# A two-layer hybrid decoder trunk on one core: paired recurrence blocks, weight slots out of turn, another load order at the start

## The chip, the cores and the metric

One core of a Trainium2 chip runs the whole program. The metric is device time in microseconds (us) from start to end. The kernel before was timed in three runs: median 1348.71 us (1348.5 to 1348.83). The profiled execution that all rows below come from took 1349.72 us.

## The reference, cut to what matters

Two layers of a trunk over 512 tokens of width 1024, all in float32. Each layer normalizes, projects the input once, sends the columns to three mixers (a chunked gated recurrence with 4 heads, latent attention, sparse attention with the 128 best keys per query), projects their outputs, adds the residual, and runs a squared-ReLU MLP of width 4096.

```python
for l in range(DEPTH):
    u = rms_norm(h, attn_norm_w[l])
    proj = u @ w_in[l]
    ...
    y_hgrn = hgrn2_mixer(hq, hf, hi, hg, lb_all[l], hgrn_norm_w[l])
    y_mla = mla_mixer(...)
    y_dsa = dsa_mixer(...)        # top-128 keys per query by an index score
    mixed = jnp.concatenate([y_hgrn, y_mla, y_dsa], axis=-1)
    h = h + mixed @ w_out[l]
    u = rms_norm(h, mlp_norm_w[l])
    h = h + jnp.square(jax.nn.relu(u @ w_mlp_in[l])) @ w_mlp_out[l]
return rms_norm(h, final_norm_w)
```

## The kernel before, in words

Activations lie transposed in eight blocks of 128 channels by 512 tokens (`h[0..7]`). A float32 product with weights is made of three products in the fast format fp32r: every operand is split into a high part (`whi`, a cast of the loaded tile `raw`, on ScalarE or VectorE) and a rest (`wlo`, a subtraction on VectorE). Weights stream through five buffers each of `raw`, `whi` and `wlo`.

Nothing is issued while the program is written: `Recorder` collects every operation with an estimated duration (`_Engine.cost`), and `order()` plans all engines at once. `forward()` is a list scheduler: at each step it takes the engine that is free first and gives it the ready operation with the most work behind it; `backward()` renews these levels from the plan just made. Twelve such rounds are run and the shortest plan is written out, so the order on every engine's queue is the planner's. Buffers are named by tags (`CAPS` says how many of each: `mm` 3 and `mx` 5 are PSUM banks, `un` 24 are general 128x512 tiles in SBUF). `RESERVE` says how many buffers of a tag must stay free before one may be taken out of its turn; 9 means strictly in turn, which holds for `raw`, `whi`, `wlo` and `mm`.

SyncE (SP) issues the loads in one queue: a load that waits for its buffer holds all behind it. The places that matter here:

- **Start** (`setup`, `vectors`): three products of zeros run on TensorE, four parts of x are loaded into `wlo` buffers, transposed by TensorE against the identity in `consts`, scaled with the first norm's rows (`an`, 16x128) and split into `u`. Positions and one norm's rows (`hnw`) are loaded from GpSimd's queue.
- **Recurrence** (`hgrn_head`, once per head and layer, 8 times): for each of four 128-token blocks, the block of products K1 x Q1 goes to the PSUM tile `pa`, and its upper right 64x64 quarter is then overwritten by Ks x Qs, a product of two 64-column operands in `hq`. VectorE copies the masked result to `at` (`copy_predicated`), TensorE multiplies `at` with the values.
- **Index top-k** (`index_topk`): 16 rounds of max and match_replace on VectorE for three query blocks, per layer.
- **Sparse attention and output projection** (`dsa_attend`, `layer`): for each of eight blocks m, 18 products over the first two mixers are accumulated in an `mm` bank, which VectorE then adds to the old `h[m]`; that was put away to DRAM (`hd[m]`) and is loaded back as `un<-d`. The sparse mixer's part (`mx<-pt` is its last product) follows in a second `mm` tile per block.

Of the kernel before, what the change touches and what calls it, by code (L numbers as in the profile page):

```python
# [22 lines left out]
DEPTH = 2  # L23
# [5 lines left out]
ROUNDS = 12  # L29
# [144 lines left out]
class Op:  # L174
    __slots__ = ("eng", "run", "dur", "lat", "preds", "succs", "bufs", "idx", "level", "left", "ready",
                 "start", "end", "window", "ways", "after", "lock")
# [7 lines left out]
class Recorder:  # L184
# [38 lines left out]
    def add(self, eng, run, outs, ins, dur, lat=0.0, lock=False):  # L223
        if self.ways is not None:
            self.ways.append((eng, run, outs, ins, dur, lat, lock))
            return None
        op = Op()
        op.lock = lock
        op.eng, op.run, op.dur, op.lat, op.idx = eng, run, dur, lat, len(self.ops)
        preds = set()  # L230
        for v in ins:
            box = v.box
            preds.update(i for i, b, w in v.buf.log if w and _meet(b, box))

        box_of = lambda v: None if eng == "PE" else v.box
        for v in outs:
            box = box_of(v)
            preds.update(i for i, b, w in v.buf.log if _meet(b, box))
        for v in outs:
            box = box_of(v)  # L240
            v.buf.log = [x for x in v.buf.log if not _within(x[1], box)] + [(op.idx, box, True)]
        for v in ins:
            if not any(v.buf is o.buf and _within(v.box, box_of(o)) for o in outs):
                v.buf.log.append((op.idx, v.box, False))
        op.bufs = list({id(v.buf): v.buf for v in list(ins) + list(outs)}.values())
        preds.discard(op.idx)
        op.window = WINDOW if lat and any(v.buf.tag in ("un", "lg") for v in outs) else 0
        op.preds, op.succs, op.ways = preds, [], None
        self.ops.append(op)
        return op  # L250

    def order(self):

        ops = self.ops
        for op in ops:
            for p in op.preds:
                ops[p].succs.append(op.idx)
        for op in reversed(ops):
            op.level = -(op.dur + op.lat + max((self.hop(op, ops[s]) - ops[s].level for s in op.succs), default=0.0))
        best = None  # L260
        for _ in range(ROUNDS):
            try:
                result, span = self.forward()
            except RuntimeError:
                if best is None:
                    raise
# [3 lines left out]
            self.backward(span)  # L270
        self.span, self.best = best[1], best[0]
        return [x[0] for x in best[0]]
# [45 lines left out]
    def forward(self):  # L318
# [25 lines left out]
        key = lambda op: (op.level, op.idx)  # L344
# [12 lines left out]
        while done < len(ops):  # L357
# [31 lines left out]
            for tag, bs in need.items():  # L389
# [4 lines left out]
                if len(s) - len(bs) < RESERVE.get(tag, 0) and max(turn[b] for b in bs) >= head[tag] + len(bs):  # L394
                    short = tag
                    break
# [39 lines left out]
            if op.lat:  # L436
                x = max(dma_free, t + 1100.0)
                dma_free = x + op.lat
                op.end = dma_free + 900.0
# [8 lines left out]
            for s in op.succs:  # L448
                o = ops[s]
                o.left -= 1  # L450
                o.ready = max(o.ready, op.end + self.hop(op, o))
# [20 lines left out]
class _Engine:  # L472
# [29 lines left out]
    def cost(self, method, named, views):  # L502
        v = dict(views)
        if method == "dma_start":
            shape = next(x for _, x in views).shape
            n = math.prod(shape) * 4
            return (60.0 if self.eng != "POOL" else 1000.0), max(100.0, n / 360.0)
        out = v.get("out") or views[0][1]
        if self.eng == "PE":
# [4 lines left out]
            if rhs.buf.r:  # L514
# [3 lines left out]
            return (130.0 if m <= 64 else 214.0), 0.0  # L518
        n = max(x.free for _, x in views)
        if self.eng == "ACT":  # L520
            d = 95.0 + n / 1.2
# [12 lines left out]
        if method == "reciprocal":  # L534
# [7 lines left out]
RESERVE = {"un": 8, "mx": 2, "t2": 2, "mm": 9, "raw": 9, "whi": 9, "wlo": 9, "sqa": 9, "rb": 9, "hw": 3, "hq": 2, "hS": 1,  # L542
           "lg": 9, "pt": 9, "u": 99}


class Build:
# [51 lines left out]
    def setup(self):  # L598
# [9 lines left out]
        nc.sync.dma_start(self.ident, a["consts"][:, 0:128])  # L608
# [8 lines left out]
        for i in range(4):  # L617
            nc.sync.dma_start(xin[i], a["x"][0, :, i * 256:(i + 1) * 256].rearrange("(t p) d -> p t d", p=128))
        self.vectors()
# [19 lines left out]

        for kt in range(KT):  # L640
# [7 lines left out]
    def vectors(self):  # L648
# [4 lines left out]
        for width, group in ((128, (("an", a["attn_norm_w"], 8),)),  # L653
# [7 lines left out]
            for key, ap, k in group:  # L661
                nc.sync.dma_start(rows[r:r + DEPTH * k, 0:width],
                                  ap.rearrange("l (k p) -> (l k) p", p=width) if k > 1 else ap)
# [9 lines left out]
        nc.gpsimd.dma_start(self.hnw, bass.AP(tensor=w.tensor, offset=w.offset, ap=[[0, 128], [128, DEPTH], [1, 128]]))  # L673
# [39 lines left out]
    def rope_tables(self):  # L713
# [3 lines left out]
        nc.gpsimd.dma_start(self.pos_i, bass.AP(tensor=pos.tensor, offset=pos.offset, ap=[[0, 128], [1, 512]]))  # L717
        self.pos_c = self.tile([128, 4], I32)
        nc.gpsimd.dma_start(self.pos_c, pos.rearrange("o (t p) -> p (o t)", p=128), allow_slow_non_contiguous=True)
# [795 lines left out]
    def hgrn_head(self, l, hd, hf, pq, vi, gate, cq, mix):  # L1515
# [187 lines left out]
```

## Time and profile before

| | us |
|---|---|
| median of three runs | 1348.71 |
| the profiled execution | 1349.72 |
| its span, first to last instruction | 1347.9 |
| TensorE busy | 1310.3 (97%) |
| VectorE busy | 1081.2 (80%) |
| ScalarE busy | 638.7 (47%) |
| mean granted TensorE clock | 0.988 |

The span has six stretches: the start to 15, the mixers of layer 0 to 310 and the rest of its output projection to 340, its MLP to 735, the same for layer 1 (mixers to 958, projection to 990), and the second MLP to 1338 with the last norm behind it. All planned operations carry one line, 491, so rows are told apart by tile names. A float32 matmul that isn't fp32r shows as two records. TensorE's ends are modelled: a stretch in which it shows as busy can still hold waits, and a gap in its row is a sure wait.

### The profile page before, as it was taken

To read this page: it belongs to the slowest core of one execution; us is meant where nothing else is said; L and a number is where in the kernel's file an instruction comes from. 1 tells how busy PE (TensorE), PEld (TensorE's weight loads), DVE (VectorE), ACT (ScalarE), POOL (GpSimd) and SP (SyncE) were. 2 spreads that over 40 slices of the span, in tenths; PEclk is the share of its full clock that TensorE was granted. 3 is DMA by queue.
4 is the path that set the end of the run, shared out by engine and by line. 5 is a ranking of instruction groups with operands and counts; after the bars stand their busy time and mean duration, and the time that the engine had idled before them with its cause. 6 is when DMAs were issued, how large, how long until landed. Compare 5 with 4: busy or idle time off the path is not lost.

```text
span 1347.9 us, 23357 instructions
## 1 busy us (share of the span) xinstructions
PE 1310.3 (97%) x9237; PEld 1185.5 (88%) x9237; DVE 1081.2 (80%) x2208; ACT 638.7 (47%) x1152; POOL 19.6 (1%) x34
## 2 busy tenths in 40 slices
PE   7999999998999999999999999999799999999996
PEld 5788788766999999999988887987599999999996
DVE  6999999984996777866666999999399777767765
ACT  5666636373553333433344684526255333433343
POOL 1010000000000000000010000000000000000000
PEclk8999999998999999999999999999899999999998
DMA  8540222333134332332463012224423223343321
GB/s 266 156 138 11 56 60 79 109 116 120 37 121 125 95 94 79 110 125 95 133 156 89 12 48 79 71 62 134 125 63 126 86 88 106 99 126 94 94 64 63
DMA packets 137106, 131.87 MB, mean 98 GB/s; under 512 B 14069, under 2 KB 129541, under 8 KB 136997
## 3 DMA queue, kind: packets, MB, share of 16 engines
q1 hardware_dynamic: 135716, 127.62, 31.1%
q0 software_dynamic: 1280, 2.77, 0.9%
q8 instruction: 72, 1.18, 0.4%
q14 instruction: 38, 0.30, 0.1%
HBM read 121.44 MB, written 8.92 MB: 97 GB/s over the span
## 4 chain that ended last, share of the span: by engine, by line
PE 88%; DVE 7%; DMA 2%; issue 1%; ACT 1%; SPq 0%; DVEq 0%; ACTq 0%
PE mm L491 58%; PE mx L491 29%; DVE un L491 3%; PE mx L1420 1%; DVE lg L491 1%; DVE wlo L491 1%; DMA wlo<-in_x_dram 1%; DMA un<-d 1%; DVE t L491 1%; DVE c L491 1%; DMA lg<-d 0%; ACT whi L491 0%; ACT t L491 0%; SPq L491 0%; ACT un L491 0%
## 5 line engine op out<-in xcount | busy, mean ns | idle before, releaser
L491 PE MATMUL mm<-un,whi 128*128 128x256 f32 (+1 forms) x2176 | 447.3, 295 | 14.8 <-DVE un L491 14.7
L491 ACT ACTIVATE whi<-raw 128x1024 fp32r<-128x1024 f32 (+2 forms) x232 | 240.6, 1041 | 413.4 <-PE mm L491 248.5
L491 PEld LDWEIGHTS mm<-un,whi 128*128 128x128 f32 x2176 | 344.5, 189 | 29.7 <-DVE un L491 16.7
L491 DVE TENSOR_TENSOR wlo<-raw,whi 128x1024 fp32r<-128x1024 f32 (+2 forms) x250 | 297.3, 1197 | 44.5 <-ACT whi L491 39.9
L491 PE MATMUL mm<-u,whi 128*128 128x512 f32 (+1 forms) x960 | 292.1, 366 | 2.1 <-DVE c L491 1.1
L491 PE MATMUL mm<-un,wlo 128*128 128x256 f32 (+1 forms) x1088 | 275.3, 294 | 0.0
L491 PEld LDWEIGHTS mm<-u,whi 128*128 128x128 f32 x960 | 176.1, 189 | 29.4 <-issue 2.9
L491 PEld LDWEIGHTS mm<-un,wlo 128*128 128x128 f32 x1088 | 190.5, 189 | 6.1 <-issue 0.8
L491 DVE TENSOR_TENSOR un<-mm,un 128x512 f32<-128x512 f32 (+2 forms) x184 | 119.8, 662 | 91.2 <-PE mm L491 77.6
L491 PE MATMUL mx<-u,whi 128*128 128x256 f32 x736 | 189.9, 282 | 0.0
L491 PE MATMUL mm<-u,wlo 128*128 128x512 f32 (+1 forms) x480 | 159.5, 363 | 0.0
L491 PE MATMUL mm<-whi,u 128*128 128x256 f32 (+1 forms) x640 | 142.2, 305 | 0.2 <-DVE un L491 0.2
L491 PEld LDWEIGHTS mx<-u,whi 128*128 128x128 f32 x736 | 137.2, 188 | 0.0
L491 PEld LDWEIGHTS mm<-whi,u 128*128 128x128 f32 x640 | 103.1, 189 | 8.0 <-issue 4.5
L491 PE MATMUL mx<-lg,whi 128*128 128x256 f32 x448 | 107.7, 281 | 0.0
L491 PE MATMUL mx<-un,un 128*128 128x512 f32 (+4 forms) x380 | 104.5, 364 | 2.0 <-DVE un L491 1.5
L491 PE MATMUL mx<-u,wlo 128*128 128x256 f32 x368 | 102.3, 282 | 0.0
L491 PEld LDWEIGHTS mm<-u,wlo 128*128 128x128 f32 x480 | 89.0, 189 | 12.0 <-issue 0.4
L491 ACT ACTIVATE un<-t 128x512 fp32r<-128x512 f32 (+1 forms) x85 | 53.3, 628 | 66.1 <-DVE t L491 60.1
L491 PE MATMUL mm<-wlo,u 128*128 128x256 f32 (+1 forms) x320 | 83.0, 299 | 0.0
L491 PEld LDWEIGHTS mx<-un,un 128*128 128x128 f32 (+1 forms) x380 | 65.2, 188 | 18.9 <-DVE un L491 4.2
L491 PEld LDWEIGHTS mx<-lg,whi 128*128 128x128 f32 x448 | 79.6, 188 | 0.0
(200 smaller groups left out, 1960.5 us busy)
## 6 DMA issues: line engine op xcount, KB each, us to landing
raw<-in_w_mlp_in_dram SPq DMA_DIRECT2D x64, 512.0 KB, 3.8
raw<-in_w_mlp_out_dram SPq DMA_DIRECT2D x64, 512.0 KB, 4.1
raw<-in_w_in_dram SPq DMA_DIRECT2D x42, 512.0 KB, 3.7
d<-un SPq DMA_DIRECT2D x20, 256.0 KB, 2.5
raw<-in_w_in_dram SPq DMA_DIRECT2D x18, 256.0 KB, 3.1
raw<-in_w_out_dram SPq DMA_DIRECT2D x16, 256.0 KB, 2.7
raw<-in_w_out_dram SPq DMA_DIRECT2D x8, 512.0 KB, 3.4
un<-d SPq DMA_DIRECT2D x16, 256.0 KB, 4.6
```

Source lines behind the costliest of these rows:

```text
L491: real(*[res(v) for v in args], **{k: res(v) for k, v in kw.items()})
L1420: self.real.tensor.matmul(outs[i].get(), vals[i].get(), rhs[i].get(), start=k == 0, stop=k == NT - 1)
```

## The change

Part by part:

1. The recurrence's four 64x64 products per head become two of 128x128, each over two blocks at once, in a PSUM tile of their own, `pz` (tag `mx`). Only the wanted quarters are copied from it into `at`, by two copies after `copy_predicated`.
2. The planner may take `raw`, `whi` and `wlo` buffers out of turn while 2 to 4 stay free (`RESERVES`, tried in turn over 24 rounds), holds fewer of `un`, `t2` and `hq` back, and has new costs: 300 for a short float32 product (130 or 214 before), 20 more for ScalarE from SBUF, a slower and later end for loads, no hop between operations of TensorE. `SEED` is 0, so the random shifts of levels are off.
3. The identity, x part 0, the rows `an` and x part 1 go first in SP's queue, in this order. Parts 2 and 3, and the loads of positions and `hnw` (now on SP), are placed by the planner.
4. Three products without a use are written behind the loads: one of x part 0, two of x part 1.

```diff
-ROUNDS = 12
+ROUNDS = 24
+SEED = 0
...
-        for _ in range(ROUNDS):
...
+        for i in range(ROUNDS):
+            for reserve in RESERVES[i % 3:]:
+                try:
+                    result, span = self.forward(reserve)
+                    break
+                except RuntimeError:
+                    continue
...
-        key = lambda op: (op.level, op.idx)
+        key = lambda op: (op.level - op.early, op.idx)
...
-                op.end = dma_free + 900.0
+                op.end = dma_free + 2200.0
...
-                o.ready = max(o.ready, op.end + self.hop(op, o))
+                o.ready = max(o.ready, op.end + (0.0 if op.eng == o.eng == "PE" else self.hop(op, o)))
...
-            return (60.0 if self.eng != "POOL" else 1000.0), max(100.0, n / 360.0)
+            return (60.0 if self.eng != "POOL" else 1000.0), max(100.0, n / 310.0)
...
-            return (130.0 if m <= 64 else 214.0), 0.0
+            return (300.0 if n < 128 else 130.0 if m <= 64 else 214.0), 0.0
...
-            d = 95.0 + n / 1.2
+            d = 95.0 + n / 1.2 + 20.0 * any(k != "out" and x.buf.tag not in PSUM_TAGS for k, x in views)
...
-RESERVE = {"un": 8, "mx": 2, "t2": 2, "mm": 9, "raw": 9, "whi": 9, "wlo": 9, "sqa": 9, "rb": 9, "hw": 3, "hq": 2, "hS": 1,
+RESERVE = {"un": 6, "mx": 2, "t2": 1, "mm": 9, "raw": 9, "whi": 9, "wlo": 9, "sqa": 9, "rb": 9, "hw": 3, "hq": 1, "hS": 1,
            "lg": 9, "pt": 9, "u": 99}
+RESERVES = [{**RESERVE, **x} for x in ({"raw": 3, "whi": 2, "wlo": 2}, {"raw": 4, "whi": 3, "wlo": 3}, {}, dict.fromkeys(RESERVE, 99))]
...
+        early = iter(range(10, 0, -1))
+        def load(out, x, **kw):
+            nc.sync.dma_start(out, x, **kw)
+            nc.ops[-1].early = 1e9 * next(early)
+        load(self.ident, a["consts"][:, 0:128])
...
-        for i in range(4):
-            nc.sync.dma_start(xin[i], a["x"][0, :, i * 256:(i + 1) * 256].rearrange("(t p) d -> p t d", p=128))
-        self.vectors()
+        x_in = lambda i, how=load: how(xin[i], a["x"][0, :, i * 256:(i + 1) * 256].rearrange("(t p) d -> p t d", p=128))
+        x_in(0)
+        self.vectors(load)
+        x_in(1)
...
+        for i in (2, 3):
+            x_in(i, nc.sync.dma_start)
+        for i, n in ((0, 1), (1, 2)):
+            for _ in range(n):
+                nc.tensor.matmul(self.ps(), xin[i][:, 0, 0:128], xin[i][:, 0:2, :], start=True, stop=True)
...
-        nc.gpsimd.dma_start(self.hnw, bass.AP(tensor=w.tensor, offset=w.offset, ap=[[0, 128], [128, DEPTH], [1, 128]]))
+        nc.sync.dma_start(self.hnw, bass.AP(tensor=w.tensor, offset=w.offset, ap=[[0, 128], [128, DEPTH], [1, 128]]))
...
+        pz = self.ps()
         for t in range(NT):
             ts = slice(t * 128, t * 128 + 128)
             nc.tensor.matmul(pa[:, ts], K1[:, ts], Q1[:, ts], start=True, stop=True)
-            nc.tensor.matmul(pa[0:64, t * 128 + 64:t * 128 + 128], Ks3[:, t, :], Qs3[:, t, :], start=True, stop=True)
...
+        for e in range(2):
+            ts = slice(e * 128, e * 128 + 128)
+            nc.tensor.matmul(pz[:, ts], Ks[:, ts], Qs[:, ts], start=True, stop=True)
...
+        z4 = pz.rearrange("p (t e j) -> p t e j", e=2, j=64)
+        for e in range(2):
+            nc.copy(at[0:64, e:4:2, 64:128], z4[e * 64:e * 64 + 64, 0:2, e, :])
```

What the planner makes of it, at three places. First SP's queue where layer 0's output projection begins; `un<-d` are the eight blocks of h that come back (`d_64` to `d_71`), `raw<-in_w_mlp_in` the first weights of the MLP. Before:

```order
L491 DMA un_3528<-d_64 128x512
L491 DMA un_3532<-d_65 128x512
L491 DMA raw_3578<-in_w_mlp_in_dram 128x4x256
L491 DMA raw_3626<-in_w_mlp_in_dram 128x4x256
L491 DMA raw_3674<-in_w_mlp_in_dram 128x4x256
L491 DMA un_3678<-d_66 128x512
L491 DMA un_3680<-d_67 128x512
L491 DMA un_3682<-d_68 128x512
L491 DMA un_3684<-d_69 128x512
L491 DMA un_3686<-d_70 128x512
L491 DMA un_3688<-d_71 128x512
```

With the change:

```order
L499 DMA un_3511<-d_64 128x512
L499 DMA un_3516<-d_65 128x512
L499 DMA un_3519<-d_66 128x512
L499 DMA un_3544<-d_67 128x512
L499 DMA raw_3598<-in_w_mlp_in_dram 128x4x256
L499 DMA raw_3622<-in_w_mlp_in_dram 128x4x256
L499 DMA raw_3640<-in_w_mlp_in_dram 128x4x256
L499 DMA un_3686<-d_68 128x512
L499 DMA un_3688<-d_69 128x512
L499 DMA un_3690<-d_70 128x512
L499 DMA un_3693<-d_71 128x512
```

Before, one MLP load stands ahead of these rows and three between the second and the third block of h; now none stands ahead, four blocks come first, and three MLP loads stand ahead of the last four. Layer 1 has the same two patterns.

Second, TensorE at the same place: the last two products of the sparse mixer (`mx<-pt`) and what stands around them; `mm<-un,whi` and `mm<-un,wlo` are the output projection, one `mm` tile per block m. Before:

```order
L1420 MATMUL mx_3610<-pt_3623,un_985 64x256
L1420 MATMUL mx_3610<-pt_3633,un_985 64x256
L491 MATMUL mm_3592<-un_3238,whi_3257 128x512
L491 MATMUL mm_3592<-un_3230,wlo_3480 128x512
L1420 MATMUL mx_3610<-pt_3637,un_985 64x128
L1420 MATMUL mx_3610<-pt_3667,un_985 64x128
L491 MATMUL mm_3692<-un_2000,whi_3221 128x512
L491 MATMUL mm_3692<-un_2176,whi_3221 128x512
L491 MATMUL mm_3692<-un_2000,wlo_3233 128x512
```

With the change:

```order
L499 MATMUL mm_3661<-un_2052,whi_3244 128x512
L1442 MATMUL mx_3625<-pt_3650,un_978 64x128
L1442 MATMUL mx_3625<-pt_3658,un_978 64x128
L499 MATMUL mm_3606<-un_3227,wlo_3187 128x512
L499 MATMUL mm_3668<-un_2052,whi_3244 128x512
L499 MATMUL mm_3661<-un_2069,whi_3244 128x512
L499 MATMUL mm_3668<-un_2069,whi_3244 128x512
L499 MATMUL mm_3661<-un_2052,wlo_3471 128x512
L499 MATMUL mm_3668<-un_2052,wlo_3471 128x512
L499 MATMUL mm_3679<-un_2052,whi_3592 128x512
L499 MATMUL mm_3661<-un_2275,whi_3244 128x512
L499 MATMUL mm_3679<-un_2069,whi_3592 128x512
```

Before, two of the three banks hold sums that wait for their add (`mm_3583` and the one closed here, `mm_3592`), and after the last `mx<-pt` each product belongs to a tile that begins here (`mm_3692`). Now one tile is open across the last `mx<-pt` (`mm_3661`), two more begin right behind it, and 53 products of these three and of `mm_3606` follow until `mm_3750` needs a bank again.

Third, TensorE in a recurrence head of layer 0; `mx<-hq,hq` are the products of the disputed quarters, `mx<-un,k` those of `at` with the values, `mm<-u,whi` the input projection. Before:

```order
L491 MATMUL mx_2923<-hw_2324,un_2234 128x128
L491 MATMUL mm_2883<-u_245,whi_2612 128x512
L491 MATMUL mx_2923<-hq_2886,hq_2414 64x64
L491 MATMUL mm_2883<-u_233,wlo_2820 128x512
L491 MATMUL mx_2923<-hw_2324,un_2234 128x128
L491 MATMUL mm_2883<-u_248,whi_2779 128x512
L491 MATMUL mx_2923<-hq_2886,hq_2414 64x64
L491 MATMUL mm_2883<-u_257,whi_2779 128x512
```

With the change:

```order
L499 MATMUL mx_2901<-hq_2863,hq_2823 128x128
L499 MATMUL mx_2903<-un_2385,hw_2818 128x128
L499 MATMUL mm_2907<-u_179,whi_2707 128x512
L499 MATMUL mx_2901<-hq_2863,hq_2823 128x128
L499 MATMUL mm_2907<-u_189,whi_2707 128x512
L499 MATMUL mm_2825<-u_312,whi_2641 128x512
L499 MATMUL mm_2907<-u_179,wlo_2763 128x512
L499 MATMUL mm_2829<-u_312,whi_2778 128x512
L499 MATMUL mx_2926<-un_2385,k_152 128x128
```

Before, each product of a quarter is a row of 64x64 in the tile of the main blocks; now two rows of 128x128 have a tile of their own (`mx_2901`), and four rows stand between the second of them and the first product that reads `at` (`mx_2926`).

## Rows read from the trace of the kernel before

**Rows 1.** Page, part 1: engine, busy us, share of the span, instructions.

```profile
PE 1310.3 (97%) x9237; PEld 1185.5 (88%) x9237; DVE 1081.2 (80%) x2208; ACT 638.7 (47%) x1152; POOL 19.6 (1%) x34
```

**Rows 2.** Stretches: length, busy us (instructions) of PE, PEld, DVE, ACT, POOL; PEclk, DMA, GB/s.

```profile
0.00:15.00 15.00, 7.77 (x21) 4.28 (x22) 4.36 (x9) 4.93 (x9) 5.28 (x13) 0.90 0.86 253
15.00:297.00 282.00, 278.22 (x1567) 226.72 (x1565) 269.02 (x754) 166.68 (x362) 7.70 (x11) 0.99 0.35 103
...
310.00:316.00 6.00, 0.25 (x3) 0.23 (x2) 1.73 (x4) 0.60 (x1) 0.00 (x0) 0.70 0.76 241
316.00:340.00 24.00, 24.00 (x99) 19.13 (x100) 15.62 (x25) 11.63 (x19) 0.00 (x0) 0.93 0.36 115
340.00:735.00 395.00, 394.30 (x3171) 384.30 (x3170) 296.51 (x421) 157.77 (x211) 5.56 (x8) 1.00 0.35 104
735.00:945.00 210.00, 207.66 (x1213) 169.08 (x1211) 201.65 (x580) 125.70 (x294) 0.00 (x0) 1.00 0.24 69
...
958.00:966.00 8.00, 1.26 (x6) 0.78 (x7) 2.54 (x4) 0.60 (x1) 0.00 (x0) 0.68 0.75 227
966.00:990.00 24.00, 24.00 (x95) 18.94 (x94) 14.60 (x24) 11.27 (x18) 0.00 (x0) 0.89 0.29 89
990.00:1338.00 348.00, 347.38 (x2955) 346.11 (x2953) 261.43 (x367) 148.01 (x213) 1.09 (x2) 1.00 0.28 88
```

**Rows 3.** Chain of waits near 310 us: start, duration, engine, operation.

```profile
307.74 1.07 ACT whi L491
...
308.83 1.24 DVE wlo L491
...
310.54 4.45 DMA un<-d
...
315.02 0.70 DVE un L491
```

**Rows 4.** Chain of waits near 958 us.

```profile
959.12 5.61 DMA un<-d
```

**Rows 5.** Timeline of SP's queue near 310 us: start, us to the last issue, transfers.

```profile
296.33 14.12 SPq L491 DMA_DIRECT2D raw<-in_w_mlp_in_dram  x3
310.54 3.09 SPq L491 DMA_DIRECT2D un<-d  x6
```

**Rows 6.** Waits in 0 to 15 us: us in total, times, longest.

```profile
PE mx L491 <- DMA wlo<-in_x_dram: 5.9, 1, 5.9
```

**Rows 7.** DMA issues in 0 to 15 us: count, KB each, us to landing.

```profile
un<-in_positions_dram POOLq DMA_DIRECT2D x1, 256.0 KB, 6.8
k<-in_hgrn_norm_w_dram POOLq DMA_DIRECT2D x1, 128.0 KB, 7.7
```

**Rows 8.** Timeline of TensorE in a recurrence head: start, us, operation.

```profile
254.91 0.33 PE L491 MATMUL mx<-hq,hq 128*64 128x64 f32 x2
255.16 0.49 PE L491 MATMUL mx<-hS,hw 128*128 128x128 f32 x2
...
258.24 0.38 PE L491 MATMUL mx<-un,k 128*128 128x128 f32 x2
258.46 0.39 PE L491 MATMUL mx<-un,hw 128*128 128x128 f32 x2
```

**Rows 9.** Waits of VectorE for `pa`, 15 to 297 us.

```profile
DVE k L491 <- PE mx L491: 3.0, 3, 1.5
```

**Rows 10.** The same, 735 to 945 us.

```profile
DVE k L491 <- PE mx L491: 1.3, 1, 1.3
```

**Rows 11.** VectorE's groups, whole span: busy us, mean ns of one, idle before.

```profile
L491 DVE TENSOR_TENSOR wlo<-raw,whi 128x1024 fp32r<-128x1024 f32 x236 | 285.6, 1218 | 36.5 <-ACT whi L491 32.3 <-PE mm L491 2.5 <-PE mx L491 0.8
...
L491 DVE CAST whi<-raw 128x1024 fp32r<-128x1024 f32 x18 | 12.4, 689 | 14.1 <-DMA raw<-in_w_in_dram 8.1 <-PE mm L491 3.8 <-PE mx L491 2.3
```

**Rows 12.** ScalarE's groups, the same columns.

```profile
L491 ACT ACTIVATE whi<-raw 128x1024 fp32r<-128x1024 f32 x218 | 229.9, 1059 | 396.0 <-PE mm L491 231.1 <-PE mx L491 134.4 <-DVE raw L491 23.6
...
L491 ACT ACTIVATE t<-mx 128x128 f32<-128x128 f32 x32 | 8.4, 275 | 12.9 <-PE mx L491 12.9
```

**Rows 13.** Timeline of TensorE at the start.

```profile
1.31 4.76 PE L491 MATMUL mx<-t 128*128 128x512 f32 x6 [1.31 <-POOL t L491]
...
12.87 0.45 PE L491 MATMUL mx<-k,wlo 128*128 128x128 f32 x1 [5.92 <-DMA wlo<-in_x_dram]
...
14.52 0.79 PE L491 MATMUL mm<-u,whi 128*128 128x512 f32 x1
```

**Rows 14.** A stretch of the start, the columns of rows 2.

```profile
12.04:18.87 6.83, 6.00 (x21) 4.33 (x21) 4.51 (x9) 4.48 (x8) 0.00 (x0) 0.50 1.09 365
```

More of the change, by code (lines that the diff above doesn't have):

```diff
@@ L28 @@
 PSUM_TAGS = ("mm", "mx")
-ROUNDS = 12
+ROUNDS = 24
+SEED = 0
+SPREAD = 50.0
 C_HQ, C_HF, C_HI, C_HG = 0, 512, 1024, 1536
@@ L175 @@
     __slots__ = ("eng", "run", "dur", "lat", "preds", "succs", "bufs", "idx", "level", "left", "ready",
-                 "start", "end", "window", "ways", "after", "lock")
+                 "start", "end", "window", "ways", "after", "lock", "early")
 ENGINES = ("PE", "DVE", "ACT", "POOL", "SP", "GQ")
@@ L227, in add @@
         op = Op()
-        op.lock = lock
+        op.lock, op.early = lock, 0.0
         op.eng, op.run, op.dur, op.lat, op.idx = eng, run, dur, lat, len(self.ops)
@@ L260, in order @@
         best = None
-        for _ in range(ROUNDS):
[L262 to L266, printed above, removed]
+        rng = np.random.default_rng(SEED)
+        for i in range(ROUNDS):
[5 more added lines that the diff above has]
+                    continue
+            else:
                 break
@@ L270, in order @@
             self.backward(span)
+            for op, x in zip(ops, rng.normal(0.0, SPREAD, len(ops)) if SEED and i > 6 else ()):
+                op.level += x
         self.span, self.best = best[1], best[0]
@@ L316, in backward, with forward @@
                     heapq.heappush(future[ops[p].eng], (at[p], p))
-    def forward(self):
+    def forward(self, reserve):
         ops = self.ops
@@ L393, in forward @@
                     break
-                if len(s) - len(bs) < RESERVE.get(tag, 0) and max(turn[b] for b in bs) >= head[tag] + len(bs):
+                if len(s) - len(bs) < reserve.get(tag, 0) and max(turn[b] for b in bs) >= head[tag] + len(bs):
                     short = tag
@@ L513, in cost @@
             n, m = rhs.free, lhs.free
-            if rhs.buf.r:
+            if rhs.buf.r or any(n == "bitcast" and x[0] == F32R for n, x, _ in rhs.steps):
                 return n * (0.4453 if n >= 256 else 1.7) + 4.0, 0.0
@@ L607, in setup @@
         self.ident = c[:, O_ID:O_ID + 128]
-        nc.sync.dma_start(self.ident, a["consts"][:, 0:128])
+        early = iter(range(10, 0, -1))
[3 more added lines that the diff above has]
+        load(self.ident, a["consts"][:, 0:128])
         self.tri = c[:, O_TRI:O_TRI + 512]
@@ L646, in setup, with vectors @@
             self.finish_h(kt, "an", 0, p)
-    def vectors(self):
+    def vectors(self, load):
         nc, a = self.nc, self.a
@@ L661, in vectors @@
             for key, ap, k in group:
-                nc.sync.dma_start(rows[r:r + DEPTH * k, 0:width],
-                                  ap.rearrange("l (k p) -> (l k) p", p=width) if k > 1 else ap)
+                (load if key == "an" else nc.sync.dma_start)(
+                    rows[r:r + DEPTH * k, 0:width], ap.rearrange("l (k p) -> (l k) p", p=width) if k > 1 else ap)
                 for l in range(DEPTH):
@@ L716, in rope_tables @@
         self.pos_i = self.un(I32)
-        nc.gpsimd.dma_start(self.pos_i, bass.AP(tensor=pos.tensor, offset=pos.offset, ap=[[0, 128], [1, 512]]))
+        nc.sync.dma_start(self.pos_i, bass.AP(tensor=pos.tensor, offset=pos.offset, ap=[[0, 128], [1, 512]]))
         self.pos_c = self.tile([128, 4], I32)
-        nc.gpsimd.dma_start(self.pos_c, pos.rearrange("o (t p) -> p (o t)", p=128), allow_slow_non_contiguous=True)
+        nc.sync.dma_start(self.pos_c, pos.rearrange("o (t p) -> p (o t)", p=128), allow_slow_non_contiguous=True)
         H = slice(64, 128)
```

## The prediction, before the result was known

> **What bounds the kernel now.** I read the busy shares first, then the busy times of each stretch, then inside the stretches where TensorE is not full the chain of waits, the waits and SP's timeline, and last the order of both kernels, for what moves.
>
> The shares say that TensorE is the bound: 1310.3 us of 1347.9 [rows 1], so it stands still for 37.6 us at most. The stretches correct this. In the two MLPs TensorE is busy 394.30 of 395 and 347.38 of 348 us [rows 2]: there nothing is to be had by better order. In the mixers it shows busy 278.22 of 282 and 207.66 of 210 us, but VectorE is at 269.02 and 201.65 in the same stretches [rows 2], and each layer's mixers end with VectorE's top-k rounds and sparse attention. VectorE is short of full by only 13.0 and 8.35 us. I take VectorE as the bound of the mixers, TensorE's small waits there as filled by its own slack; whoever shortens a TensorE product in a head wins nothing by it.
>
> Three sure gaps remain. At the start TensorE is busy 7.77 of 15 us [rows 2]. At 310 it is busy 0.25 of 6 us, at 958 it is busy 1.26 of 8 us, and behind each gap the granted clock is below full for a while: 0.93 over 24 us, 0.89 over 24 us [rows 2].
>
> **Gaps at the output projections.** The chain shows why TensorE stands still at 310: a cast on ScalarE at 307.74, the split on VectorE at 308.83, then at 310.54 the load of a block of h, 4.45 us, and VectorE's add at 315.02 [rows 3]. SP's timeline has the link between the split and the load: three MLP weight loads are issued from 296.33 on and the last only 14.12 us later, since they wait for a `raw` buffer that this split frees, and the six loads of h stand behind them in the queue, from 310.54 [rows 5]. All three `mm` banks hold sums that wait for these adds. Layer 1 shows the same link, with a load of 5.61 us from 959.12 on [rows 4].
>
> The price: TensorE is idle 6.00 - 0.25 = 5.75 us and 8.00 - 1.26 = 6.74 us [rows 2]. The lower clock behind costs 24 x 0.07 = 1.7 and 24 x 0.11 = 2.6 us [rows 2]. Together 16.8 us.
>
> With the change four blocks of h are loaded ahead of the first MLP weights, instead of two, and 53 products follow between the last sparse product and the first need of another bank. In the stretch behind the gap 99 matmul records take 24 us at a clock of 0.93 [rows 2], about 0.23 us each at full clock, so the cover is some 12 us, against loads of 4.45 and 5.61 us. Three MLP loads still stand ahead of the last four blocks of h, so what is late next is the add of `mm_3661`, if a `raw` buffer comes free later than 12 us after the last sparse product; that it does is rival A. I take the whole 16.8 us; bounds 0 and -16.8.
>
> **Start.** TensorE waits 5.9 us for the second part of x [rows 6]; it lands at 12.87, and the first product with weights is at 14.52 [rows 13]. With the change 384 KB that GpSimd's queue loads at the same time [rows 7] go behind on SP, and the weights of 512 KB that stood ahead of x part 1 come after it. The stretch moves 253 GB/s [rows 2]; 384 KB are 1.5 us of that. With the 512 KB it would be 896 KB, 3.5 us; but the weights then land later, and the first product needs them too. I take -1.5, bounds 0 and -3.5.
>
> The three idle products: six records of zeros at the start, two to a product of 512 columns, take 4.76 us [rows 13], 1.6 us a product. One of the new ones stands in the wait for x part 1. The other two stand behind the first four products with weights, where TensorE next needs `wlo` from VectorE; if it would not have to wait there, they cost 2 x 1.6 = 3.2. On the other side stands the clock. After the idle 5.9 us the granted clock is 0.50, which is 1.2 GHz, from 12.04 to 18.87, and TensorE is busy for 6.00 us of it [rows 14]; at 2.4 GHz it would need half, so the idle product in the wait can win up to 3.0. I take 0 for the three together, bounds -3.0 and +3.2, since the two other falls of the clock follow 5.75 and 6.74 us of idle time, and no row shows one product in such a gap. The Trainium skill, page "TensorE: Matmul & The Clock Gate", section "What's actually happening", says that the throttled state is the default and that activity releases it. By that rule the product in the wait should hold the clock, and the term would be -3.0 instead of 0. The trace agrees as far as every fall of the clock in these rows follows a gap.
>
> **Paired blocks.** On TensorE a head loses four 64-column products and gains two of 128. The timeline gives 0.25 us from such a product to the next one's start (254.91 to 255.16) and 0.22 for 128 columns (258.24 to 258.46) [rows 8]: 4 x 0.25 - 2 x 0.22 = 0.56 us a head, 4.5 us over eight heads. It lies beside VectorE's work in the mixers, so I count 0; bounds 0 and -4.5.
>
> Added: two copies a head on ScalarE, 16 in all, each at most the 0.275 us of a copy of 128 columns [rows 12], 4.4 us in all. ScalarE is busy 166.68 of 282 and 125.70 of 210 us [rows 2], which hides them, unless they are late: rival C. VectorE issues nothing more for it.
>
> Where pairing may touch the bound: VectorE's masked copy waits for the products in `pa`, three times 3.0 us together in layer 0 [rows 9] and 1.3 us in layer 1 [rows 10]. Four products instead of eight now fill `pa`, and the planner knows their price better. I take all 4.3 us away; bounds 0 and -4.3.
>
> **Work that moves between engines.** Up to the end of each layer's sparse attention only VectorE's own work counts. In layer 0 the order has 713 instructions of it up to there instead of 706. The largest pieces are two more casts of weights at 0.689 us and one `wlo` split of 1.218 us less [rows 11]; with one more copy and a few short ones I get +1.8. In layer 1 it is 500 instead of 501, -0.1. Sum +1.7, bounds 0 and +3.
>
> **Buffers out of turn, in the MLPs.** TensorE is full there with the old order, so nothing is to be won. Could it lose? In the order the weight loads stand as far ahead of their first product as before. Taken 0, bounds -1 and +2.
>
> **The sum.** -16.8 - 1.5 - 4.3 + 1.7 = -20.9. The profiled execution took 1349.72 us, so 1328.8; the median of the runs shown is 1.0 below it, which gives 1327.8, called **1328**.
>
> **Rivals.**
>
> *A. The gaps stay.* The planner only thinks that the loads come in time: it knew a latency before, too, and TensorE stood still. For it: three MLP loads still wait in the same queue ahead of four blocks of h. Against: 12 us of cover where before there was none. Then only -1.5 - 4.3 + 1.7 = -4.1 remain: 1344.6. With one of the two gaps (half of 16.8) 1336.
>
> *B. More than that.* VectorE is idle 13.0 + 8.35 - 4.3 = 17.0 us more in the mixers. TensorE's 4.5 us a program, and an order from 24 rounds, may close half of it: 8.5 us, 1319. All of it would be 1311. For it: the waits are many and short, for products. Against: no single one is touched by the edits.
>
> *C. Slower: the product with `at` waits for ScalarE.* The new copies have to pass what ScalarE has begun. A cast of weights takes 1.059 us [rows 12]; behind one cast and two copies `at` is late by 1.6 us a head, behind two casts by 2.67. In the head shown only four rows, some 0.9 us at 0.23, stand between. TensorE's row then holds everything behind it, VectorE's input too. At 1.6 us a head this costs 12.8 us: 1340.6. At 2.67 it costs 21.4, which eats the whole gain: 1349. Slower by over 0.2% needs 20.9 + 2.7 = 23.6 us, 2.95 us a head, so two casts and a further operation each time, or two casts while one output projection's gap stays. Against it: the planner costs ScalarE's copy, and orders both engines from one plan; only a wrong cost makes it late.
>
> *D. The start goes another way.* If the idle products hold the clock, their term is -3.0: 1324.8. For it: the gap is cut in two. Against: what stands after it waits for x parts 2 and 3 as well. If they do not do what they say and only delay, the start loses 3.2 us instead of winning 1.5: +4.7, 1332.5.
>
> **How the numbers follow.** Forecast 0.54, B 0.14, A 0.12 (half of it with one gap left), C 0.12, D 0.08 (half each way). 0.2% is 2.7 us, about what a measurement of this kernel can tell from no change, so faster means below 1346.0 and slower above 1351.4. Forecast, B and D are faster. Of A 0.02 is same, where both gaps stay and nothing else is won. Of C 0.02 is faster, 0.03 same and 0.07 slower: an order that is wrong for ScalarE in one head is likely wrong in all eight. So 0.88 faster, 0.05 same, 0.07 slower. The range reaches from 1313, near B's end, to 1342, which takes in D, C at one cast a head and A with one gap left. Outside stay A with both gaps (0.06), most of C (0.10) and B's end (0.02), 0.18 together.
>
> **What would show it.** Right: no idle stretch above 2 us on TensorE in the two output projections and a granted clock of 1.00 there; `un<-d` loads on SP that are issued before the last sparse product; waits of `k` for `mx` on VectorE under 2 us in all; first product with weights near 13 us; the top-k and sparse attention of layer 0 ending some 4 us earlier and the second MLP as long as before. Wrong: an idle stretch of TensorE behind the 53 products with `un<-d` as its releaser (A); waits of TensorE for `k` from ScalarE, of over a us in each head (C); VectorE with less than 15 us idle over both mixers (B); MLPs longer than 395 and 348 us, which no rival here explains.

## The result, and the profile after

The changed kernel takes 1326.02 us (median of 4 runs, 1325.49 to 1328.85), the kernel before, run beside it, 1348.77 us. The ratio is 0.9834 with a 95% interval of 0.9817 to 0.9851: 22.4 us less by the ratio. Forecast were 1328 us and 20.9 us less. The profiled execution took 1326.39 us, its span is 1324.5 us.

The first part of the page, against [rows 1]:

```profile
PE 1305.8 (99%) x9211; PEld 1189.3 (90%) x9211; DVE 1074.8 (81%) x2210; ACT 637.9 (48%) x1166; POOL 17.8 (1%) x31
```

VectorE and ScalarE did nearly as much as before. TensorE is busy 4.5 us less and stands still 1324.5 - 1305.8 = 18.7 us instead of 37.6. These two differences, -4.5 and -18.9, are the 23.4 us by which the span is shorter. The first is no smaller amount of work: at the lower level of the clock (granted 0.50) TensorE was busy for 15.2 us before (6.00 from 12.04, 3.5 from 312.41 and 5.7 from 960.95 us on) and is for 3.4 us now (from 12.88 on). Half of the difference, 5.9 us, is an estimate of what the clock gave back; by it TensorE has 1.4 us more to do than before at full clock, the three products without a use among it. The stretches show where the idle time went (columns as in [rows 2]; layer 1 now ends earlier, so its limits differ):

```profile
0.00:15.00 15.00, 10.83 (x31) 5.78 (x32) 6.69 (x12) 7.91 (x13) 3.46 (x10) 0.93 0.60 181
15.00:297.00 282.00, 276.48 (x1564) 226.16 (x1564) 271.06 (x760) 164.85 (x364) 7.63 (x11) 1.00 0.36 108
...
310.00:316.00 6.00, 6.00 (x27) 4.86 (x26) 1.91 (x3) 1.06 (x1) 0.00 (x0) 1.00 0.27 81
316.00:340.00 24.00, 24.00 (x143) 20.84 (x143) 22.92 (x44) 14.98 (x28) 0.00 (x0) 1.00 0.30 88
...
735.00:930.00 195.00, 193.31 (x1144) 159.26 (x1143) 192.18 (x566) 119.11 (x283) 0.00 (x0) 1.00 0.23 68
...
945.00:960.00 15.00, 15.00 (x66) 12.11 (x65) 7.82 (x13) 4.85 (x8) 0.00 (x0) 1.00 0.30 94
960.00:977.00 17.00, 17.00 (x112) 15.40 (x112) 17.00 (x38) 11.50 (x22) 0.00 (x0) 1.00 0.31 93
977.00:1317.00 340.00, 340.00 (x2868) 339.78 (x2867) 251.19 (x345) 135.13 (x200) 1.11 (x2) 1.00 0.28 89
```

TensorE is busy 6.00 of 6 us from 310 on, and 15.00 of 15 and 17.00 of 17 us at layer 1's output projection, at full clock. Both gaps of [rows 2] are gone, 12.5 us of idle time. At the start it is busy 10.83 instead of 7.77 us: 3.1 more. The last norm, from TensorE's last product to the end of the span, takes 7.1 us (1317.4 to 1324.5) instead of 10.4 (1337.5 to 1347.9): 3.3. Together that is 18.9. In 15 to 297 us TensorE shows 5.5 us of idle time against 3.8 before; the MLPs and layer 1's mixers make up for it.

One thing went the other way. These are the MLPs, from the end of the output projection's last product to the MLP's last product, layer 0 and layer 1, first in the kernel before and then with the change:

```profile
342.20:687.40 345.20, 345.05 (x2922) 343.05 (x2922) 267.38 (x350) 136.96 (x177) 5.56 (x8) 1.00 0.34 105
992.90:1337.50 344.60, 344.49 (x2940) 343.61 (x2938) 258.23 (x359) 145.42 (x209) 1.09 (x2) 1.00 0.28 88
```

```profile
331.10:677.80 346.70, 346.70 (x2918) 346.31 (x2917) 259.18 (x341) 142.51 (x185) 4.54 (x7) 1.00 0.33 103
968.00:1317.40 349.40, 349.40 (x2946) 348.97 (x2944) 260.59 (x370) 140.80 (x211) 1.11 (x2) 1.00 0.28 88
```

With nearly the same products, all at full clock, the MLPs take 1.5 and 4.8 us longer, 6.3 together, and TensorE shows no idle time in them. The 2880 products of their second half (`mm<-un,whi` and `mm<-un,wlo` with 256 columns) follow each other every 0.119 us on average, every 0.116 us before.

SP's queue at layer 0's output projection, against [rows 5] (start, us to the last issue, transfers):

```profile
293.91 4.78 SPq L499 DMA_DIRECT2D raw<-in_w_mlp_in_dram  x3
299.17 3.98 SPq L499 DMA_DIRECT2D un<-d  x4
```

All eight blocks of h are issued by 303.2 us; the last sparse product ends at 302.8 instead of 310.0. Before, six of them were issued from 310.54 on.

TensorE at the start, against [rows 13]:

```profile
10.00 1.07 PE L499 MATMUL mx<-k,wlo 128*128 128x128 f32 x8 [1.42 <-DMA wlo<-in_x_dram]
12.50 1.78 PE L499 MATMUL mm<-u,whi 128*128 128x512 f32 x4 [1.44 <-ACT whi L499]
```

The wait for x part 1 is 1.42 us instead of 5.92; the next wait, 1.44 us, is for the cast of the first weights on ScalarE. The first product with weights starts at 12.50 instead of 14.52.

VectorE's masked copies of `pa`, in the whole span (columns as in [rows 11]). Their waits were 3.0 and 1.3 us in [rows 9] and [rows 10]; 0.5 us is left, at the first copy of layer 0, and none in layer 1:

```profile
L499 DVE COPY_PREDICATED k<-k,mx 128x512 f32<-128x512 uint8 x8 | 5.8, 731 | 0.5 <-PE mx L499 0.5
```

### The profile page after: what moved, and what is told of

Same layout as the page of the kernel before. It is cut to its first block, busy times and chain, and to the rows that moved or that the text cites. A ratio compares the mean times of both kernels' runs of the same rounds, so it can differ in the third digit from the quotient of the medians.

```text
span 1324.5 us, 23334 instructions
## 1 busy us (share of the span) xinstructions
PE 1305.8 (99%) x9211; PEld 1189.3 (90%) x9211; DVE 1074.8 (81%) x2210; ACT 637.9 (48%) x1166; POOL 17.8 (1%) x31
## 4 chain that ended last, share of the span: by engine, by line
PE 86%; DVE 8%; DMA 2%; ACT 2%; issue 1%; SPq 0%; DVEq 0%; ACTq 0%
PE mm L499 56%; PE mx L499 29%; DVE un L499 3%; PE mx L1442 2%; DMA raw<-in_w_in_dram 1%; DVE wlo L499 1%; DVE lg L499 1%; DVE c L499 1%; DVE t L499 1%; DVE hw L499 1%; ACT un L499 1%; DMA d<-un 1%; ACT t L499 0%; ACT whi L499 0%; SPq L499 0%
## 5 line engine op out<-in xcount | busy, mean ns | idle before, releaser
L499 ACT ACTIVATE whi<-raw 128x1024 fp32r<-128x1024 f32 (+3 forms) x224 | 231.9, 1041 | 371.0 <-PE mm L499 191.7
L499 PE MATMUL mm<-u,whi 128*128 128x512 f32 (+1 forms) x960 | 285.6, 360 | 2.3 <-ACT whi L499 1.4
L499 PE MATMUL mx<-u,whi 128*128 128x256 f32 x736 | 179.5, 281 | 0.0
L499 PE MATMUL mm<-whi,u 128*128 128x256 f32 (+1 forms) x640 | 146.7, 303 | 1.5 <-ACT un L499 1.3
L499 PEld LDWEIGHTS mx<-u,whi 128*128 128x128 f32 x736 | 132.8, 189 | 0.0
L499 PE MATMUL mx<-lg,whi 128*128 128x256 f32 x448 | 105.0, 281 | 0.0
L499 PE MATMUL mm<-wlo,u 128*128 128x256 f32 (+1 forms) x320 | 89.2, 304 | 0.0
```

Source lines behind the costliest of these rows:

```text
L499: real(*[res(v) for v in args], **{k: res(v) for k, v in kw.items()})
```

## The experiments

In seven runs (all seeds among them) the planner makes a new order; in the other five the order of the changed kernel, or of the kernel named, stays as it is on every engine and only the edit stands in it. A kernel is compared with the changed one through its ratio to the kernel before, which ran on the same chip in each call.

**One thing moved in the kernel before** (`e5_before_blocks_early`). After planning, in each layer:

```diff
+            hold = [x for x in plan if x[3] in loads[2:]]
+            plan = [x for x in plan if x not in hold]
+            k = next(i for i, x in enumerate(plan) if x[3] == loads[1])
+            plan[k + 1:k + 1] = hold
```

> The kernel before in its own order on every engine, with one thing moved: in SP's queue the last six loads of h of each layer stand ahead of the three or four MLP weight loads instead of behind them. Theory (the gaps come from that queue alone): both gaps of 5.75 and 6.74 us and the slower clock behind them go, 16.8 us: 1332.0. Rival A (the adds are late for another reason, or the MLP weights are now late instead): less than half, 1340 to 1349.

Measured: 1335.68 us, ratio 0.9909 (0.9894 to 0.9924), 12.3 us less. SP's queue, TensorE's next product after the last sparse one, and VectorE just ahead of it:

```profile
290.04 3.84 SPq L504 DMA_DIRECT2D un<-d  x8
294.78 37.24 SPq L504 DMA_DIRECT2D raw<-in_w_mlp_in_dram  x7
```

```profile
310.52 1.11 PE L504 MATMUL mm<-un,whi 128*128 128x512 f32 x2 [2.05 <-DVE un L504]
```

```profile
307.28 1.22 DVE L504 TENSOR_TENSOR wlo<-raw,whi 128x1024 fp32r<-128x1024 f32 x1 [7.71 <-ACT whi L504]
309.18 0.69 DVE L504 TENSOR_TENSOR un<-mx,un 128x512 fp32r<-128x512 f32 x1 [0.67 <-ACT un L504]
309.78 1.87 DVE L504 TENSOR_TENSOR un<-mm,un 128x512 f32<-128x512 f32 x3
```

The loads now come 20 us earlier, and yet TensorE waits 2.05 us (1.62 us in layer 1, idle stretches in brackets). The adds (`un<-mm,un`, from 309.78) have their blocks of h, but stand on VectorE behind a `wlo` split and behind `un<-mx,un`, which needs the last sparse product. So the queue of SP was the cause of most of the gaps, and VectorE's own order, by the trace, of the rest. The clock, behind the first gap and around the second:

```profile
312.00:316.00 4.00, 4.00 (x15) 3.17 (x14) 1.11 (x1) 1.06 (x1) 0.00 (x0) 0.74 0.00 0
...
952.00:960.00 8.00, 6.38 (x29) 4.85 (x30) 4.30 (x6) 1.66 (x2) 0.00 (x0) 1.00 0.26 72
```

Behind the gap of 2.05 us it still falls, to 0.74 over 4 us; behind the one of 1.62 us it stays.

**The number that put the loads forward.** One of the planner's numbers is enough, in both kernels, to change how many blocks of h go ahead: the `un` buffers held back.

```diff
-RESERVE = {"un": 8,
+RESERVE = {"un": 6,
```

> The kernel before with one number of the planner changed, planned anew: 6 instead of 8 buffers of un are held back. In its order SP loads four blocks of h ahead of the MLP weights, as in the changed kernel, and a tile of mm is open across the last sparse product. Theory (this number alone put the loads of h forward, and the gaps came from them): gaps gone, 12 to 17 us less, 1331 to 1336. Rival (the gaps went by the later end that the planner gives to loads, or by slots out of turn): within 5 of 1348.

Measured in the kernel before: 1347.85 us, ratio 1.0001 (0.9992 to 1.0009). The forecast of this run was wrong: TensorE's gaps shrink from 5.75 and 6.74 to 1.65 us each, and nothing is gained. In the new order the last sparse product of layer 0 ends at 317.6 instead of 310.0 us, that of layer 1 at 965.9 instead of 958.3: products of the projection that stood behind the gap now stand before it. What the gaps gave is lost in the MLPs of this order, in the same stretches as above:

```profile
338.00:687.60 349.60, 348.48 (x2920) 346.74 (x2919) 264.96 (x346) 140.81 (x183) 5.59 (x8) 1.00 0.35 105
986.60:1335.90 349.30, 348.37 (x2938) 347.33 (x2936) 257.31 (x358) 143.60 (x211) 1.09 (x2) 1.00 0.28 87
```

They take 4.4 and 4.7 us longer than in the kernel before, 9.1 together, against 9.2 us that the gaps lost. Why the products of the MLPs run slower in a new order was not tried. All the other new orders have it too, 346.0 us or more in layer 0 and 348.7 or more in layer 1, also with the slots strictly in turn (`e6_in_turn`: 346.7 and 350.0); `e5_before_blocks_early`, in the old order, has not (345.0 and 344.5).

> The changed kernel with the old number, 8 buffers of un held back, planned anew. In its order SP loads two blocks of h, then three or four MLP weights, then six blocks, as in the kernel before. Theory: an idle stretch of some 4 to 7 us on TensorE in each output projection is back, with the slower clock behind it: 1336 to 1343. Rival (the later end of loads or the slots out of turn closed the gaps): 1323 to 1331.

The other way round, with 8 in the changed kernel: 1355.11 us, ratio 1.0051 (1.0038 to 1.0064), 29 us slower than the changed kernel and slower than the kernel before. The gaps are back, and TensorE waits at the start of the MLPs as well (the first products of the projection behind the gap, and of layer 0's MLP):

```profile
312.09 1.22 PE L499 MATMUL mm<-un,whi 128*128 128x512 f32 x2 [4.86 <-DVE un L499]
```

```profile
363.01 1.01 PE L499 MATMUL mm<-u,whi 128*128 128x256 f32 x3 [1.97 <-DVE u L499]
```

The gap in layer 1 is 5.83 us. The wait at the MLP is for `u`, the MLP's input from VectorE; the next expectation has it wrong, as a wait for weights. Then, in this kernel's own order, the loads of h moved as in `e5_before_blocks_early`:

> The kernel of run e13_after_un8 in its own order, with one thing moved: in SP's queue the last six loads of h of each layer stand ahead of the MLP weight loads. Theory (by the trace of that run 17 of its 29 us over the changed kernel are its two gaps and the slower clock behind them, the other 12 are waits for the first MLP weights): the gaps shrink to 2 us each as in e5_before_blocks_early, 12 us less, 1343; 1331 if the waits at the start of the MLPs go too. Rival (the loss has no link with SP's queue): 1350 or more.

Measured: 1345.03 us, ratio 0.9969 (0.9956 to 0.9981), by the ratios 11.1 us less than `e13_after_un8`. The gaps shrink to 1.38 and 2.04 us, the waits at the MLPs' starts stay. The two runs that move only the loads agree: 12.3 and 11.1 us.

**Slots in turn, and other orders.**

```diff
-RESERVES = [{**RESERVE, **x} for x in ({"raw": 3, "whi": 2, "wlo": 2}, {"raw": 4, "whi": 3, "wlo": 3}, {}, dict.fromkeys(RESERVE, 99))]
+RESERVES = [RESERVE, RESERVE, RESERVE, dict.fromkeys(RESERVE, 99)]
```

> The changed kernel with raw, whi and wlo buffers taken strictly in turn again, planned anew; all else as changed. Its order still loads four blocks of h ahead. Theory (slots out of turn are worth nothing, TensorE being full in the MLPs): 1326, within 4 for another order. Rival (they are what lets VectorE and SP run ahead): 1335 or more.

Measured: 1330.90 us, ratio 0.9868 (0.9856 to 0.9881), some 4.5 us slower than the changed kernel. By itself that can't be told from another order, as the next run shows (`SEED = 1`):

> The changed kernel with the planner's random shifts on (seed 1), which gives another order of the same work; it also loads four blocks of h ahead. It shows how far the time moves by the order alone: within 4 of 1326.0 by the theory that the gaps, VectorE's work and TensorE's work in the heads set the time; 1335 or more if the changed kernel's order were a lucky one.

Measured: 1339.35 us, ratio 0.9934 (0.9922 to 0.9946). The expectation was wrong: the same work in another order costs 13 us. The trace has idle stretches of 2.89 and 2.77 us at the two output projections, though four blocks of h are loaded ahead. What differs in the order is the cover: how many products of the projection that need only the first two mixers stand behind the last sparse product and ahead of the first that needs the sparse mixer. From this three more seeds were chosen, by the order alone:

> The changed kernel with random shifts in the planner, seed 5. In its order only 7 and 5 products of the output projection that need nothing of the sparse mixer are left behind the last sparse product of a layer, before the first product that needs it; seed 1 had 6 and 10, the changed kernel 55 and 61. Theory (these products are the cover, and without them TensorE stands still): an idle stretch of 1.5 to 3 us in each output projection, with a slower clock behind it, 1334 to 1343. Rival (the number plays no part): as the changed kernel, 1323 to 1330, or scattered alike for all seeds.

> As seed 5, with seed 7: 59 and 52 such products are left as cover. Theory: no idle stretch over 0.5 us on TensorE in either output projection, 1322 to 1331. Rival: 1334 or more, as with seed 1.

> As seed 5, with seed 8: 57 and 59 such products are left as cover. Theory: no idle stretch over 0.5 us on TensorE in either output projection, 1322 to 1331. Rival: 1334 or more, as with seed 1.

| kernel | cover, layers 0 and 1 | idle there, us | median, us | ratio to before |
|---|---|---|---|---|
| changed | 55, 61 | none | 1326.02 | 0.9834 |
| `e16_seed8` | 57, 59 | 0.26, none | 1321.61 | 0.9795 |
| `e16_seed7` | 59, 52 | none, 1.36 | 1332.02 | 0.9868 |
| `e6_in_turn` | 57, 7 | none, 2.77 | 1330.90 | 0.9868 |
| `e16_seed5` | 7, 5 | 2.77, 2.81 | 1333.28 | 0.9879 |
| `e8_seed1` | 6, 10 | 2.89, 2.77 | 1339.35 | 0.9934 |
| `e12_before_un6` | 4, 6 | 1.65, 1.65 | 1347.85 | 1.0001 |

The kernel before has a cover of 38 and 39 by this count, but its banks are full and the adds wait for loads. The gaps of the seeds came as forecast: with under 12 products of cover each layer has one of 1.65 to 2.89 us, with over 50 none of the kind (seed 7's 1.36 us lie before the last sparse product). In seed 5 three products of the cover run behind the last sparse product of layer 0; then TensorE waits 2.77 us for VectorE:

```profile
315.38 1.22 PE L499 MATMUL mm<-un,whi 128*128 128x512 f32 x2 [2.77 <-DVE un L499]
```

```profile
312.42 0.69 DVE L499 TENSOR_TENSOR un<-mx,un 128x512 fp32r<-128x512 f32 x1 [8.24 <-ACT un L499]
313.49 1.23 DVE L499 TENSOR_TENSOR wlo<-raw,whi 128x1024 fp32r<-128x1024 f32 x1 [0.39 <-ACT whi L499]
314.64 1.88 DVE L499 TENSOR_TENSOR un<-mm,un 128x512 f32<-128x512 f32 x3
```

`un<-mx,un` is the rest of the sparse mixer's output; the adds of the finished tiles stand behind it and behind a split. With cover TensorE works through this, as the two projections of seed 8 show:

```profile
299.00:330.00 31.00, 30.74 (x142) 24.69 (x139) 22.30 (x35) 14.48 (x25) 0.00 (x0) 1.00 0.43 136
930.00:960.00 30.00, 30.00 (x134) 22.67 (x133) 17.36 (x26) 12.65 (x22) 0.00 (x0) 1.00 0.49 157
```

The times were forecast less well: seed 5 lies 0.7 us below its range, seed 7 1.0 us above. Seed 7 has three idle stretches of 1.04, 1.69 and 1.32 us between 48 and 56 us, and its granted clock is 0.50 from 53 to 59 us; the changed kernel has one of 1.59 us there and keeps its clock. Which of the order's choices make such stretches was not tried. Seed 8 is faster than both kernels of this document: 1321.61 us, ratio 0.9795 (0.9782 to 0.9808).

**The three products without a use,** left out of the changed kernel:

> The changed kernel in its own order on every engine, only the three products without a use are left out. Theory (they are worth nothing, as in the sum): 1326.0 us, within 1. Rival (they hold the clock): the granted clock of the stretch 12.04 to 18.87 falls from 0.75 to 0.50, some 6 us of products there take half as long again, and the time is 1.5 to 2 us more, 1327.5 to 1328. Second rival (they only delay): up to 3 us less, 1323.

```diff
-        return [x[0] for x in best[0]]
+        return [x[0] for x in best[0] if x[3] not in self.drop]
...
+                nc.drop.add(nc.ops[-1].idx)
```

Measured: 1326.18 us, ratio 0.9841 (0.9826 to 0.9855). The same stretch without them and with them:

```profile
12.04:18.87 6.83, 6.57 (x19) 4.33 (x19) 5.69 (x12) 4.62 (x9) 0.00 (x0) 0.53 0.69 229
```

```profile
12.04:18.87 6.83, 6.37 (x19) 3.62 (x19) 4.92 (x8) 4.10 (x7) 0.00 (x0) 0.75 0.59 193
```

They do hold the clock up, 0.75 instead of 0.53. Over 9 to 20 us the mean granted clock is 0.69 in all four kernels without them (the kernel before, `e5_before_blocks_early`, `e12_before_un6` and this run) and 0.84 to 1.00 in the ten with them. But no gain in time is measured: the ratios differ by less than their intervals, some 2 us. In this profile the first product with weights starts at 11.60 instead of 12.50 us.

**TensorE's time in a head.** In the changed kernel's order each product of pairs is issued as two of 64x64, and the copies into `at` read both from rows 0 to 63 of `pz`:

```diff
+            def quarters(e=e, pz=pz, Ks3=Ks3, Qs3=Qs3):
+                for t in (2 * e, 2 * e + 1):
+                    nc.nc.tensor.matmul(pz[0:64, t * 64:t * 64 + 64].get(), Ks3[:, t, :].get(), Qs3[:, t, :].get(),
+                                        start=True, stop=True)
+            nc.ops[-1].run = quarters
...
-            nc.copy(at[0:64, e:4:2, 64:128], z4[e * 64:e * 64 + 64, 0:2, e, :])
+            nc.copy(at[0:64, e:4:2, 64:128], z4[0:64, 0:2, e, :])
```

> The changed kernel in its own order; only each of the two 128x128 products of a recurrence head is issued as two products of 64x64 into the same tile, as many as the kernel before had. TensorE gets the 0.56 us a head back, 4.5 us over eight heads. Theory (VectorE bounds the mixers, TensorE's saving there is off the path): 1326.0, within 1. Rival (work of TensorE that doesn't fit into the mixers is only pushed behind them, so that its sum counts): 1330.5.

Measured: 1329.96 us, ratio 0.9874 (0.9854 to 0.9894); the interval lies above that of the changed kernel, but barely, since the four runs fall into two pairs (1327.6 twice, 1332.3 and 1332.7). The trace is the surer measure. In a head, and the same place of the changed kernel:

```profile
185.59 0.45 PE L1606 MATMUL mx<-hq,hq 128*64 128x64 f32 x4
185.97 0.49 PE L499 MATMUL mm<-u,whi 128*128 128x512 f32 x1
```

```profile
187.66 0.39 PE L499 MATMUL mx<-hq,hq 128*128 128x128 f32 x2
187.80 0.48 PE L499 MATMUL mm<-u,whi 128*128 128x512 f32 x1
```

Two quarters back to back take 0.38 us to the next product, a pair 0.14. Summed over the 16 places from start to next start it is 5.6 against 2.7 us, so TensorE got 2.8 us more, not 4.5. The first `match_replace` of layer 0's top-k starts 2.15 us earlier than in the changed kernel, which lies at the start, and the end comes 1.24 later, 3.4 us in between. Instruction by instruction the two traces drift apart only where the heads are: by 1.9 us from 181 to 283 us and by 1.4 from 814 to 917, and by under 0.1 between and behind them. What TensorE does in a head counts in full.

**VectorE's time in a head.** The masked copy is issued twice:

```diff
+        once = nc.ops[-1].run
+        nc.ops[-1].run = lambda: (once(), once())
```

> The changed kernel in its own order; only VectorE's masked copy of a recurrence head is issued twice in a row, with the same result: 0.734 us more on VectorE in each of eight heads, 5.9 us together. Theory (VectorE bounds the mixers): 1331.9, or down to 1330 where the second copy falls into an idle moment. Rival (TensorE's sum of work bounds, VectorE has room): within 1 of 1326.0.

Measured: 1333.39 us, ratio 0.9893 (0.9878 to 0.9909), by ratio 8 us slower than the changed kernel.

```profile
L499 DVE COPY_PREDICATED k<-k,mx 128x512 f32<-128x512 uint8 x16 | 11.7, 732 | 0.7 <-PE mx L499 0.5
```

16 copies of 0.732 us instead of 8: 5.9 us more. From the first `match_replace` of the top-k to the end the span is 5.8 us longer, and again the drift lies in the heads (2.9 and 3.0 us in the same two stretches). VectorE's time counts in full too.

## Why the prediction was right, and where its steps were not

**The gaps, -16.8.** The mechanism was right: the loads of h stood behind MLP weights in SP's queue. With only the loads moved it is worth 12.3 us in the kernel before, 73% of the term, and 11.1 in the other order, because VectorE's adds are late for a second reason. In the changed kernel the gaps vanish, since four blocks of h go ahead and 55 and 61 products cover the rest; both were named. What a closed gap gives can be lost again in the order that closes it: in `e12_before_un6` the gaps shrank by 9.2 us, the MLPs grew by 9.1 and the time stayed.

**Paired blocks, taken as 0.** This step failed. "It lies beside VectorE's work in the mixers, so I count 0" is refuted by `e2_four_quarters`: 2.8 us more on TensorE cost 3.4 us by the trace. The sum of the pairing, 4.5 us, was small rather than wrong: from start to next start the 32 quarters took 8.3 us before, the 16 pairs take 2.7, some 5.5 less. That VectorE bounds the mixers was right as far as its own time counts in full (`e3_masked_twice`); wrong was that then TensorE's can't. In a head the two wait for each other in turn: that this is why both count is my reading, and no run separates it.

**VectorE's waits, -4.3, and its moved work, +1.7.** The waits of the masked copies fell from 4.3 to 0.5 us, 3.8 of the 4.3 taken. The moved work shows as 2.0 us more that VectorE is busy from 15 to 297 us (271.06 against 269.02). The seeds show orders of the same work 18 us apart, so what terms of this size gave in time can't be read out of a replanned kernel.

**Buffers out of turn, in the MLPs, taken 0, bounds -1 and +2.** This step failed too. "TensorE is full there with the old order, so nothing is to be won" overlooks that a full TensorE can be slower: the MLPs take 6.3 us longer. It is not the slots out of turn that do it, since `e6_in_turn` and `e12_before_un6` have it without them; the cause stays open.

**Start, -1.5.** The first product with weights came 2.0 us earlier, but the first `match_replace` of the top-k only 0.3 (101.87 to 101.58), and the `max` ahead of it 2.8 later (97.87 to 100.66). Nor does one profile measure it: `e5_before_blocks_early` has the start of the kernel before, and there the first product is at 12.68 instead of 14.52; in `e12_before_un6`, which nearly has it, at 11.16. What the load order is worth stays open.

The Trainium skill, page "TensorE: Matmul & The Clock Gate", section "What's actually happening", has activity release the throttle. The granted clock of 0.53 without and 0.75 with the idle products agrees with it. By it the time should have fallen by up to 3 us; `e1_no_idle` measured none.

**Not in the sum:** the last norm, 3.3 us shorter. All kernels planned with the new numbers have it at 7.0 to 7.9 us, the three planned with the old ones at 10.4 to 10.6. That it comes from the planner is my reading. It is neither the number for `un` (10.6 in `e12_before_un6`, 7.4 in `e13_after_un8`) nor the slots out of turn (7.9 in `e6_in_turn`); the others were not tried.

So the number came out near for partly wrong reasons: what pairing and the last norm gave beyond the sum, some 5.5 + 3.3 us, and the 6.3 us that the new order took back in the MLPs nearly cancel. That they do is luck. Two of the signs named as right did not come: the top-k of layer 0 does not end earlier (its last `match_replace` starts at 250.09 instead of 247.81 us; only the last sparse product ends 7.2 us earlier), and the second MLP is not as long as before. Longer MLPs were named as a sign of being wrong that no rival explains; it came, and is still unexplained.

Of the rivals, A's gaps are gone, and C never came: TensorE has no wait for `k` from ScalarE in either stretch of the mixers. B is not out. Its sign, VectorE less than 15 us idle over both mixers, came (282 - 271.06 and 195 - 192.18, 13.8 us, the second over a shorter stretch than before). Without the 6.3 us of the MLPs the time would be 1319.7, by estimate, where B put it at 1319; no run separates B's mechanism from the pairing and the last norm.

## What to carry to other kernels

When a load that is needed soon shares a queue with loads that wait for buffers, moving it ahead was a measurable gain by itself here (12.3 and 11.1 us); look then at which engine's queue holds the next instruction up, and count the independent products that cover it. In a kernel whose order a planner makes, change one thing with the order held fixed to price it, and run a few seeds to learn how far order alone moves the time: here a gain of 22 us stands beside a scatter of 18. Compare the stretches in which an engine is full as well: the same products took 6.3 us longer there. An engine that is short of idle time does not make the other engines' time free.

## What was not expected of the hardware

- A float32 product with 64 columns costs more by its neighbours than by itself: alone between other products it takes 0.26 us from start to next start, back to back two take 0.38, while one of 128 columns takes 0.14 to 0.22.
- The granted clock fell to 0.74 over 4 us behind an idle stretch of 2.05 us, and not behind one of 1.62 us (`e5_before_blocks_early`). The length of the stretch alone does not tell: in `e12_before_un6` it fell behind both stretches of 1.65 us, to 0.58 from 320 to 324 and 0.57 from 969 to 973 us.
- Products of one kind, at full clock on a TensorE without idle time, follow each other every 0.116 us in one order of the program and every 0.119 in another (the second half of the MLPs).
- The same start, instruction for instruction, reached its first product with weights at 14.52 and at 12.68 us in two profiles.
